# Four more weight blocks as seven products, and a solve whose transposes stay on VectorE

## The chip, the cores and the metric

The kernel runs on one core of a Trainium2 chip. The metric is the time of one execution on the device in microseconds (us). Its engines run side by side: TensorE (PE, with its weight loads as PEld), VectorE (DVE), ScalarE (ACT), GpSimd (POOL) and SyncE (SP). SP, ACT and POOL each have a queue that issues DMAs in order.

## The reference

One residual layer on 1024 tokens of width 1024. A normalised input h is projected by one wide matrix; two mixers use the parts, and gates join them:

```python
h = _rmsnorm(x, norm_w[layer])
proj = h @ w_in[layer]
dsa_qkv, dsa_z, gdn_qkv, gdn_z, gdn_b, gdn_a, gate_a, gate_b = _split_columns(proj)
...
o_a = _dilated_mixture(q_a, k_a, v_a)            # three groups of dilated window attention
y_a = (o_a * silu(dsa_z)) @ w_up_a[layer]
cqkv = silu(_causal_depthwise_conv(gdn_qkv, conv_w[layer]))      # 4 taps
gq, gk, gv = split(cqkv)                          # l2 norms on gq, gk
o_b = _gated_delta_rule(gq, gk, gv, g, beta)      # chunks of 64, a scan over 16 chunks
y_b = (_rmsnorm(o_b, gdn_norm_w) * silu(gdn_z)) @ w_up_b[layer]
merged = sigmoid(gate_a) * y_a + sigmoid(gate_b) * y_b
x = x + merged @ w_out[layer]
return _rmsnorm(x, final_norm_w)
```

In each chunk of the delta rule a unit lower triangular 64x64 matrix I + A has to be inverted for each head: t_inv = (I + A)^-1, A from the keys, beta and the decays.

## The kernel before

**Projections.** The wide matrix is cut into units of 256 columns: 18 of attention (query, key and value for three groups and two halves of the heads), 6 of the delta rule ("gdn", a half of the heads `hb` and query, key or value), 4 of z and 8 of the gates. fp32 accuracy comes from fp16 pairs: h is h_hi + h_lo, a weight block whi + wlo, and three matmuls (hi·hi, lo·hi, hi·lo; lines L184, L185, L186) make one product. A unit is done in one of two ways:
- *Normal*: four output tiles of 128 columns x 512 tokens, each 8 slices of depth x 3 matmuls of 512 columns. ScalarE makes whi (L167), VectorE wlo (L84, 128x1024), twice each. A unit is 32 steps ("ticks") of three matmuls.
- *Seven*: the unit as a 2x2 matrix of blocks, multiplied in seven products of half the depth instead of eight (a Strassen scheme, with the sums of h made once). 28 ticks. VectorE makes four sums of weight blocks (L329), and seven low halves (L84, 128x512), ScalarE seven high ones (L330). Two of the four outputs come out as -p - rest and need a pass of VectorE when they leave PSUM.

`SEVENS` lists the units done the second way.

**Order.** PE's instructions stand in the order in which the code writes them: a queue `feed` of units gives projection matmuls, and the other work calls `feed.tick(n)` to put n ticks of them between its own steps. The numbers of ticks (`STATE_LAG`, `tick(2)` and others) are set by hand. The order on all other engines, DMA issues among them, is set by a planner at the end of the program (`Step.cost`, `fill`), which goes through the program with a table of durations and fixes one order per engine. Engines wait in that order.

**After the attention** come, with the remaining units between the steps: `decay` (products gm, then exp), `keys_side` (key norms, pair products MT, and the scalars brk and rk packed for the solve), `solve`, `merge`, `state_parts`, for hb = 0 and 1, then query pairs, the scan over chunks, and the up and output projections. `solve` inverts 32x32 blocks: MT goes to DRAM and comes back as As with one matrix in each partition (4 row blocks x 32 matrices), 31 steps of two VectorE instructions (stmp, X) give the inverse X, and X goes back through DRAM (u_d) into MT. A transposed negative copy T goes through DRAM (t_d) into T1p. `merge` joins the 32x32 blocks to 64x64 on PE: left products of MT and T1p (L1353), a VectorE pass Y, right products of Y and U (L1368). The scalars `bsc` reach the solve by a PE transpose, a copy and two DMA passes through DRAM (sc_d).

**Keys.** `rope_out` copies rotated queries and keys out of their tiles into Q and K by DMAs of 32 partitions, high halves (pch, pkh) and low halves (pcl, pkl), all on SP's queue. POOL's queue carries the weight loads wstage.

Of the kernel before, what the change touches and what calls it, by code (L numbers as in the profile page):

```python
# [11 lines left out]
F32 = mybir.dt.float32  # L12
# [18 lines left out]
U_Z = 24  # L31
# [7 lines left out]
def gdn_unit(hb, what):  # L39
    return U_GDN + hb * 3 + what  # L40
# [5 lines left out]
          + [U_GATE + i for i in (0, 1, 2, 6, 7)] + [U_Z + i for i in range(4)])  # L46
# [11 lines left out]
STATE_LAG = 12  # L58
# [20 lines left out]
def hybrid_block(ctx: ExitStack, tc: tile.TileContext, A):  # L79
# [544 lines left out]
    def rope_out(pt, pieces):  # L624

        with tc.high_priority():
            for name, dst, r0, _ in pieces:
                for hd in range(4):
                    nc.sync.dma_start(out=dst[r0:r0 + 32, hd], in_=pt[name[1]][32 * hd:32 * hd + 32, "AB".index(name[0])])
# [366 lines left out]
    def conv_unit(hb, what, dst_of, then=None):  # L996

        def gen(w):
            for c in range(2):
# [3 lines left out]
                for hf in range(2):  # L1003
                    def take(p):
                        with tc.high_priority():
# [8 lines left out]
                            for j in (2, 1, 0):  # L1014
                                STT(a, xc[:, j:j + 512], cw[:, cidx, j:j + 1], a, ALU.mult, ALU.add)
                            parts = [(dst[:, 8 * hf:8 * hf + 8].rearrange("p c i -> p (c i)"), lambda x: x)]
                            if hb:

                                dv = dst[:, 8 * hf:8 * hf + 8].rearrange("p (t c) i -> p t c i", c=2)
                                parts = [(dv[:, :, b], lambda x, b=b: x.rearrange("p (t c i) -> p t c i", c=2, i=64)[:, :, 1 - b])  # L1020
                                         for b in range(2)]
                            if (hb, what) in SILU:
                                for d, of in parts:
                                    SC.activation(d, of(a), AF.Silu, scale=2.0)
                            else:
                                th = pre[0].tile([128, 512], F32, name="cth", tag="cth", bufs=2)
                                SC.activation(th, a, AF.Tanh)
                                for d, of in parts:
                                    STT(d, of(th), 1.0, of(a), ALU.add, ALU.mult)
# [6 lines left out]
        feed.add(("gdn", hb, what), Normal(A["w"][gdn_unit(hb, what)]), gen)  # L1036
# [145 lines left out]
    def decay(hb):  # L1182

        for t in range(8):
# [18 lines left out]
            feed.tick(2)  # L1203
# [23 lines left out]
    def sumsq(hb, src, dst, take=None):  # L1227

        for t0 in range(0, 8, 2):
# [11 lines left out]
            feed.tick(2)  # L1241
# [36 lines left out]
    def keys_side(hb):  # L1278
# [7 lines left out]
        for i, x in enumerate((brk, rk)):  # L1286
            V.tensor_copy(pack[:, i].rearrange("p t (e q) -> p t e q", e=2), heads_h2(x[:, :, hsl]))
# [20 lines left out]
    def solve(hb, m_d, bsc):
# [8 lines left out]
        for k in range(31):  # L1317
# [8 lines left out]
        V.tensor_scalar(T1, X.rearrange("p j i -> p i j"), -1.0, None, op0=ALU.mult)  # L1326
        u_d = tc.dram_tile([4, 32, 32, 32], F32, name=f"u_d{hb}")
        t_d = tc.dram_tile([4, 32, 32, 32], F32, name=f"t_d{hb}")
        nc.sync.dma_start(out=u_d.rearrange("k n j i -> (k n) (j i)"), in_=X.rearrange("p j i -> p (j i)"))
        nc.sync.dma_start(out=t_d.rearrange("k n j i -> (k n) (j i)"), in_=T1.rearrange("p j i -> p (j i)"))  # L1330
        U = MT[hb]
        T1p = p2_.tile([128, 8, 4, 32], F32, name="T1p", tag="T1p", bufs=1)
        for kb in range(4):
            b = kb % 2
            if b == 0:
                nc.sync.dma_start(out=T1p[32 * kb:32 * kb + 32].rearrange("p t h j -> p (t h) j"),
                                  in_=t_d[kb].rearrange("n i j -> i n j"))
# [129 lines left out]
    gate_unit(5, gate_spill)  # L1467
# [52 lines left out]
    for i in (6, 7):  # L1520
        gate_unit(i, gate_spill)
# [257 lines left out]
    feed.until(("gate", 6))  # L1779
# [179 lines left out]
QUEUE_NS = 4  # L1959
# [47 lines left out]
class Step:  # L2007
# [17 lines left out]
    def cost(self):  # L2025
# [17 lines left out]
        elif self.kind == "InstDMACopy":  # L2043
            kb = w[0].total / 1024
            rows = max(x.rows[1] - x.rows[0] for x in self.args)
            self.hold = 590 if rows <= 32 else 500 if rows <= 64 else 350
            self.ns, self.pass_ns, self.kb = 2800 + (4 if w[0].dram else 7) * kb, 60, kb
            if min(w[0].piece, r[0].piece) < 256:
                self.hold = 1400 if kb > 64 else 600
                self.ns += 2800  # L2050
            if self.eng == "POOL":
                self.hold = 530 if rows > 64 else 630
        elif self.eng == "DVE":
            one = len(r) == 1
            fast = one and not r[0].psum
            self.ns = {"InstMemset": 60 + 0.5 * n, "InstReciprocal": 150 + 6.2 * n, "InstTensorCopy": 160 + (0.55 if fast else 1.0417) * n}.get(
# [109 lines left out]
def fill(steps, rank, back, given):  # L2166
# [4 lines left out]
    free, moved, due, open_ = [{e: x() for e in order} for x in (float, float, list, list)]  # L2171
# [201 lines left out]
```

## Time and profile before

| | us |
|---|---|
| median of 3 runs (1048.63 to 1051.87) | 1049.8 |
| the profiled execution | 1048.82 |
| its span, first to last instruction | 1047.0 |
| PE busy | 1029.0 (98%) |
| VectorE busy | 885.7 (85%) |
| ScalarE busy | 583.0 (56%) |
| POOL busy | 56.1 (5%) |

The granted TensorE clock was 0.998. A matmul row has the time until its last result is written, and rows overlap, so PE's busy share says that it always has something in flight, not that it runs at its peak. The profile is of one execution, and the stages it names are read by the time from the span's start.

### The profile page before, as it was taken

The numbers are of one execution on the slowest core, as the hardware profiler recorded it, in microseconds if no ns is written. First come the engines' busy times: TensorE is split into PE (matmuls) and PEld (weight loads), VectorE is DVE, ScalarE is ACT, GpSimd is POOL, SyncE is SP. The second block draws the span as 40 slices with busy tenths as digits, with TensorE's granted clock in tenths as the row PEclk, the third lists the DMA queues.
The fourth block names the chain that finished last, engine by engine and source line by source line (L and its number), as shares of the span: only waits on it lengthen the run. The fifth ranks groups of instructions, "written<-read, shape, count | busy, mean of one in ns | idle before, by whom it ended". The sixth has DMA issues, their size and how long they took to land.

```text
span 1047.0 us, 24924 instructions
## 1 busy us (share of the span) xinstructions
PE 1029.0 (98%) x9962; PEld 632.9 (60%) x9962; DVE 885.7 (85%) x2052; ACT 583.0 (56%) x1322; POOL 56.1 (5%) x107
## 2 busy tenths in 40 slices
PE   6999999999999999999999999999999999999997
PEld 5995595775966855876655545545555555444444
DVE  6898988979979889989998897976588768899934
ACT  6455767777767766667756633344444345344523
POOL 0000000000000000010010000110100001000000
PEclk9999999999999999999999999999999999999999
DMA  8144531542624622470146357794874415743232
GB/s 284 64 129 114 138 112 62 152 112 78 186 84 116 165 91 74 118 201 28 43 161 183 113 134 202 258 278 150 266 254 152 142 62 176 288 124 117 67 115 81
DMA packets 99780, 148.53 MB, mean 142 GB/s; under 512 B 31168, under 2 KB 64704, under 8 KB 98512
## 3 DMA queue, kind: packets, MB, share of 16 engines
q1 hardware_dynamic: 69264, 84.64, 27.9%
q0 software_dynamic: 12320, 44.11, 13.4%
q10 hardware_dynamic: 18080, 18.20, 5.0%
q8 instruction: 78, 1.28, 0.5%
q14 instruction: 38, 0.31, 0.1%
HBM read 91.13 MB, written 36.90 MB: 122 GB/s over the span
## 4 chain that ended last, share of the span: by engine, by line
PE 84%; DVE 10%; ACT 2%; DMA 1%; issue 1%; SPq 0%; DVEq 0%; ACTq 0%
PE ps_mm L184 21%; PE ps_mm L186 20%; PE ps_mm L185 20%; PE ps_G L813 2%; PE ps_S L186 2%; PE ps_S L185 2%; PE ps_S L184 2%; DVE ca L84 1%; PE ps_S L790 1%; PE ps_S L792 1%; PE ps_G L185 1%; PE ps_G L186 1%; PE ps_G L184 1%; DVE sm L799 1%; DVE tl L87 1%
## 5 line engine op out<-in xcount | busy, mean ns | idle before, releaser
L186 PE MATMUL ps_mm<-h_hi,wlo 128*128 128x512 f16 (+1 forms) x504 | 189.3, 376 | 0.0
L184 PE MATMUL ps_mm<-h_hi,whi 128*128 128x512 f16 (+1 forms) x436 | 163.8, 376 | 0.0
L185 PE MATMUL ps_mm<-h_lo,whi 128*128 128x512 f16 (+1 forms) x436 | 163.5, 375 | 0.0
L186 PEld LDWEIGHTS <-wlo 128*128 128x128 f16 x748 | 73.2, 98 | 81.4
L184 PEld LDWEIGHTS <-whi 128*128 128x128 f16 x816 | 79.9, 98 | 65.7
L185 PEld LDWEIGHTS <-whi 128*128 128x128 f16 x816 | 79.9, 98 | 64.4
L803 ACT ACTIVATE sm<-sm,osb 128x128 f32<-128x128 f32 (+1 forms) x160 | 69.3, 434 | 34.9 <-DVE osb L799 33.3
L330 ACT ACTIVATE whi<-wstage 128x512 f16<-128x512 f32 x84 | 51.1, 626 | 30.0 <-DVE wstage L329 11.9
L799 DVE CUSTOM_DVE_ANT_0 sm<-ps_S,amask 128x128 f32<-128x128 f32 (+1 forms) x192 | 60.3, 345 | 6.6 <-PE ps_S L792 6.5
L87 DVE TENSOR_TENSOR tl<-ps_G,th 128x256 f16<-128x256 f32 (+1 forms) x96 | 51.7, 539 | 13.3 <-ACT th L818 13.0
L84 DVE SCALAR_TENSOR_TENSOR whi<-wstage,whi 128x512 f16<-128x512 f32 x84 | 57.2, 684 | 4.6 <-ACT whi L330 4.4
L329 DVE TENSOR_TENSOR wstage<-wstage 128x512 f32<-128x512 f32 x84 | 56.9, 685 | 0.8
L185 PE MATMUL ps_mm<-wlo,h_hi 128*128 128x256 f16 (+1 forms) x256 | 57.3, 246 | 0.0
L84 DVE SCALAR_TENSOR_TENSOR ca<-xc,cw,ca 128x512 f32<-128x512 f32 x72 | 53.7, 745 | 3.8 <-ACT ca L1013 3.3
L184 PE MATMUL ps_mm<-h_hi,wlo 128*128 128x512 f16 x136 | 51.6, 380 | 0.0
L185 PE MATMUL ps_mm<-h_lo,wlo 128*128 128x512 f16 x136 | 51.5, 379 | 0.0
L84 DVE SCALAR_TENSOR_TENSOR wlo<-wstage,whi 128x1024 f16<-128x1024 f32 x38 | 46.1, 1218 | 6.3 <-ACT whi L167 5.6
L818 ACT CAST th<-ps_G 128x256 f16<-128x256 f32 (+1 forms) x96 | 44.0, 458 | 12.5 <-PE ps_G L813 10.8
L813 PE MATMUL ps_G<-cons,sm 128*128 128x128 f32 x280 | 46.9, 274 | 1.3 <-ACT sm L803 1.2
L84 DVE SCALAR_TENSOR_TENSOR wlo<-wstage,wlo 128x512 f16<-128x512 f32 x63 | 42.4, 683 | 6.2 <-ACT wlo L330 6.2
L313 POOL DMA_DIRECT2D wstage<-in_w x42 | 22.2, 530 | 473.2 <-DVE whi L84 154.9
L184 PE MATMUL ps_mm<-whi,h_hi 128*128 128x256 f16 (+1 forms) x192 | 46.5, 256 | 0.0
(492 smaller groups left out, 2950.3 us busy)
## 6 DMA issues: line engine op xcount, KB each, us to landing
wstage<-in_w POOLq DMA_DIRECT2D x68, 512.0 KB, 4.5
og<-osb ACTq DMA_DIRECT2D x32, 132.0 KB, 2.2
og<-og SPq DMA_DIRECT2D x32, 132.0 KB, 2.4
sga<-gspa SPq DMA_DIRECT2D x8, 512.0 KB, 9.1
wstage<-in_w_up POOLq DMA_DIRECT2D x8, 512.0 KB, 5.3
sgb<-gspb SPq DMA_DIRECT2D x8, 512.0 KB, 4.2
wos<-in_w_out SPq DMA_DIRECT2D x8, 512.0 KB, 4.7
xr<-in_x SPq DMA_DIRECT2D x8, 512.0 KB, 4.1
```

Source lines behind the costliest of these rows:

```text
L84: (eng or V).scalar_tensor_tensor(out, in0, scalar, in1, op0=op0, op1=op1)
L87: (eng or V).tensor_tensor(out, in0, in1, op)
L184: PE.matmul(out, lhsT=wh(k), rhs=mh(k), start=first and i == 0, stop=False, skip_group_check=True)
L185: PE.matmul(out, lhsT=wh(k), rhs=ml(k), start=False, stop=False, skip_group_check=True)
L186: PE.matmul(out, lhsT=wl(k), rhs=mh(k), start=False, stop=last and i == len(ks) - 1, skip_group_check=True)
L313: nc.gpsimd.dma_start(out=st, in_=self.src[n])
L329: V.tensor_tensor(self.part[name], self.part[x], self.part[y], ALU.add)
L330: SC.activation(t[:, b, 0], self.part[name], AF.Copy, scale=W_SCALE)
L799: V.tensor_tensor_reduce(P[:, u, :128 * nk], psc[:, u * 256:u * 256 + 128 * nk], mask, -cexp, -NEG, ALU.add, ALU.min, accum_out=osb[:, 256 ...
L803: SC.activation(P[:, u, :128 * nk], P[:, u, :128 * nk], AF.Exp, bias=osb[:, 256 + hd:257 + hd], scale=-1.0, accum_out=osb[:, 260 + hd:261 ...
L813: PE.transpose(pt[:, c:c + 128], P[:, u, i * 128:i * 128 + 128], ident)
L818: SC.copy(th[:, :n], pt[:, :n])
```

## The change

Five parts, in one diff:
1. Four more units become *Seven*: gates 3, 4 and 5 and the gdn query unit of hb = 1. For the latter `conv_unit` gets a `gen7`; the filter's part is moved into a function. Gate 6 moves ahead of the z units. The numbers of ticks are made fewer by 16 in `decay`, `sumsq` and `STATE_LAG`, as the four units have 16 ticks fewer.
2. T1p is written by one VectorE transpose of 32x32 blocks from X; T, t_d and its DMAs are gone. The sign is put into brk (times -1) and the solve's step adds.
3. bsc is written by a VectorE transpose from pack; the PE transpose, packT, sc_d and its DMAs are gone.
4. The pieces of U come back in the order 1, 3, 0, 2. Low key pieces are issued by POOL instead of SP.
5. The planner's table: one DMA path shared by all queues instead of one for each, with other prices, and a price for the transpose.

```diff
 SEVENS = ([att_unit(g, hs, w) for g in (1, 0) for hs in range(2) for w in range(3)]
-          + [U_GATE + i for i in (0, 1, 2, 6, 7)] + [U_Z + i for i in range(4)])
+          + [gdn_unit(hb, w) for hb, w in [(1, 0)]] + [U_GATE + i for i in (0, 1, 2, 3, 4, 5, 6, 7)] + [U_Z + i for i in range(4)])
-STATE_LAG = 12
+STATE_LAG = 8
...
-                    nc.sync.dma_start(out=dst[r0:r0 + 32, hd], in_=pt[name[1]][32 * hd:32 * hd + 32, "AB".index(name[0])])
+                    eng = nc.gpsimd if name[1] == "l" and not twice else nc.sync
+                    eng.dma_start(out=dst[r0:r0 + 32, hd], in_=pt[name[1]][32 * hd:32 * hd + 32, "AB".index(name[0])])
...
+        def gen7(w):
+            dst, edge, held = {}, {}, []
+
+            def shifted(c, hf, p, rest):
+                xc = pre[0].tile([128, 515], F32, name="xc", tag="xc", bufs=2)
+                if hf == 0:
+                    V.memset(xc[:, 0:3], 0.0)
+                if rest is None:
+                    SC.copy(xc[:, 3:515], p)
+                else:
+                    STT(xc[:, 3:515], p, -1.0, rest, ALU.mult, ALU.subtract)
+                ...
+            yield from seven_products(w, out)
+        add_unit(("gdn", hb, what), gdn_unit(hb, what), gen, gen7)
...
-            feed.tick(2)                       # decay
+            feed.tick(2 - (hb ^ (t > 3)))
-            feed.tick(2)                       # sumsq
+            feed.tick(1 + hb)
...
-            V.tensor_copy(pack[:, i].rearrange("p t (e q) -> p t e q", e=2), heads_h2(x[:, :, hsl]))
+            V.tensor_scalar(pack[:, i].rearrange("p t (e q) -> p t e q", e=2), heads_h2(x[:, :, hsl]),
+                            (-1.0, 1.0)[i], None, op0=ALU.mult)
+        bsc = p2_.tile([128, 2, 32], F32, name="bsc", tag="bsc", bufs=2)
+        V.transpose(bsc.rearrange("p a i -> p (a i)"), pack.rearrange("p a t h -> p (a t h)"))
...
-        PE.transpose(pp[0:64, 0:128], pack.rearrange("p a t h -> p (a t h)"), ident)
-        SC.copy(packT, pp[0:64, 0:128])
-        ... sc_d written and read by three DMAs
...
-            TT(X[:, :k + 1, k + 1:], X[:, :k + 1, k + 1:], tv, ALU.subtract)
+            TT(X[:, :k + 1, k + 1:], X[:, :k + 1, k + 1:], tv, ALU.add)
         TT(X, X, bsc[:, 1, None, :].to_broadcast([128, 32, 32]), ALU.mult)
-        T1 = p2_.tile([128, 32, 32], F32, name="T1", tag="As", bufs=1)
-        V.tensor_scalar(T1, X.rearrange("p j i -> p i j"), -1.0, None, op0=ALU.mult)
-        ... t_d written and read by three DMAs
+        T1p = p2_.tile([128, 8, 4, 32], F32, name="T1p", tag="T1p", bufs=1)
+        V.transpose(T1p.rearrange("p t h j -> p j (t h)"), X)
-        for kb in range(4):
+        for kb in (1, 3, 0, 2):
...
-QUEUE_NS = 4
-            self.ns, self.pass_ns, self.kb = 2800 + (4 if w[0].dram else 7) * kb, 60, kb
+            self.kb = max(3.07 * kb, 1.6 * w[0].total / min(w[0].piece, r[0].piece))
+            self.ns, self.pass_ns = 3000 + 1.3 * self.kb, 60
-            moved[e] = max(moved[e], t) + s.kb * QUEUE_NS
+            moved = max(moved, t + 2000) + s.kb
```

The end of the solve of hb = 0 on VectorE; ca and vT belong to the filter of a value unit, which runs beside it. Before:

```order
L87 TENSOR_TENSOR stmp<-As,X 128x60
L87 TENSOR_TENSOR X<-X,stmp 128x30x2
L87 TENSOR_TENSOR stmp<-As,X 128x31
L87 TENSOR_TENSOR X<-X,stmp 128x31
L87 TENSOR_TENSOR X<-X,bsc 128x1024
L84 SCALAR_TENSOR_TENSOR ca<-xc,cw,ca 128x512
L1326 TENSOR_SCALAR T_9060<-X 128x1024
L84 SCALAR_TENSOR_TENSOR ca<-xc,cw,ca 128x512 x2
```

After:

```order
L87 TENSOR_TENSOR X<-X,stmp 128x31
L87 TENSOR_TENSOR X<-X,bsc 128x1024
L84 SCALAR_TENSOR_TENSOR ca<-xc,cw,ca 128x512
L1363 STREAM_TRANSPOSE T1p<-X 128x32x32
L87 TENSOR_TENSOR rv<-ps_O,bg 128x512
L84 SCALAR_TENSOR_TENSOR ca<-xc,cw,ca 128x512
L87 TENSOR_TENSOR As<-As,bsc 128x1024
```

The transpose stands where T stood, and the next solve's first instruction (As) follows it three places on.

SP's queue at the same place: u_d and t_d are the ways of X and T out, MT and T1p their ways back, As the matrices of the next solve, rv_d values on their way to DRAM. Before:

```order
L1329 DMA u_d_9062<-X 128x1024
L1330 DMA t_d_9063<-T_9060 128x1024
L1338 DMA MT_8581<-u_d_9062 32x32x32
L1336 DMA T1p<-t_d_9063 32x32x32 x2
L1338 DMA MT_8581<-u_d_9062 32x32x32
L1311 DMA As<-m_d_9433 128x1024
```

After:

```order
L1348 DMA As<-m_d_9376 128x1024
L1365 DMA u_d_9015<-X 128x1024
L1485 DMA rv_d<-rv 128x4x128
L1369 DMA MT_8581<-u_d_9015 32x32x32 x4
L1426 DMA rvt<-rv_d 128x4x256
```

As is now issued ahead of u_d, and T's three issues are gone.

POOL's queue about the last key block (Ks; L313 are loads of Seven units, L163 of Normal ones). Before:

```order
L313 DMA wstage<-in_w 128x1024 x26
L163 DMA wstage<-in_w 128x1024 x4
L313 DMA wstage<-in_w 128x1024 x4
L163 DMA wstage<-in_w 128x1024 x2
L1315 MEMSET X 128x1024
```

After:

```order
L313 DMA wstage<-in_w 128x1024 x6
L163 DMA wstage<-in_w 128x1024 x3
L630 DMA Ks<-pcl 32x1024 x8
L163 DMA wstage<-in_w 128x1024
L313 DMA wstage<-in_w 128x1024 x4
L163 DMA wstage<-in_w 128x1024
```

The eight low pieces of that key block stand behind the third of four loads of Normal units.

More of the change, by code (lines that the diff above doesn't have):

```diff
@@ L1013, in take @@
                             SC.activation(a, p, AF.Copy, scale=cw[:, cidx, 3:4])
[L1014 to L1029, printed above, removed]
+                            filtered(c, hf, xc, a, dst, cidx)
                         last.append(xc)
@@ L1034, in gen, with finish, out @@
                     yield from proj(w, c, hf, take)
-        feed.add(("gdn", hb, what), Normal(A["w"][gdn_unit(hb, what)]), gen)
+        def gen7(w):
[6 more added lines that the diff above has]
+                    SC.copy(xc[:, 3:515], p)
+                else:
+                    STT(xc[:, 3:515], p, -1.0, rest, ALU.mult, ALU.subtract)
+                if hf == 0:
+                    edge[c] = pre[0].tile([128, 4], F32, name="edge", tag="edge", bufs=2)
+                    V.tensor_copy(edge[c][:, 0:3], xc[:, 512:515])
+                return xc
+            def finish(c, hf, xc):
+                cidx = 4 * what + 2 * hb + c
+                if c not in dst:
+                    dst[c] = dst_of(c)
+                if hf:
+                    V.tensor_copy(xc[:, 0:3], edge[c][:, 0:3])
+                a = pre[0].tile([128, 512], F32, name="ca", tag="ca", bufs=2)
+                SC.activation(a, xc[:, 3:515], AF.Copy, scale=cw[:, cidx, 3:4])
+                filtered(c, hf, xc, a, dst[c], cidx)
+                if hf and then:
+                    then(c, dst[c])
+            def out(c, hf, p, rest):
+                with tc.high_priority():
+                    xc = shifted(c, hf, p, rest)
+                    if (c, hf) == (1, 1):
+                        held.append(xc)
+                        return
+                    finish(c, hf, xc)
+                    if (c, hf) == (1, 0):
+                        finish(1, 1, held[0])
+            yield from seven_products(w, out)
+        add_unit(("gdn", hb, what), gdn_unit(hb, what), gen, gen7)
     kT, pre = [], []
@@ L1778, in hybrid_block @@
             feed.tick(4)
-    feed.until(("gate", 6))
+    feed.until(("z", "b", 1))
     feed.tick(1)
@@ L2170, in fill @@
     start, order = [0.0] * len(steps), {e: [] for e in ENGINES.values()}
-    free, moved, due, open_ = [{e: x() for e in order} for x in (float, float, list, list)]
+    free, due, open_ = [{e: x() for e in order} for x in (float, list, list)]
+    moved = 0.0
     events, wake, table, small, end = [], {}, 0, None, 0.0
@@ L2234, in fill @@
         if s.kb and not back:
-            moved[e] = max(moved[e], t) + s.kb * QUEUE_NS
-            late = max(0, moved[e] + 1200 - t - s.ns)
+            moved = max(moved, t + 2000) + s.kb
+            late = max(0, moved + 300 - t - s.ns)
         end = max(end, t + late + s.ns)
```

47 lines of the change are left out of this document (25 added, 22 removed).

## The prediction

> **What bounds the kernel now.** I read the page first, its busy line and the shares of the chain that ended last:
>
> ```profile
> PE 1029.0 (98%) x9962; PEld 632.9 (60%) x9962; DVE 885.7 (85%) x2052; ACT 583.0 (56%) x1322; POOL 56.1 (5%) x107
> PE 84%; DVE 10%; ACT 2%; DMA 1%; issue 1%; SPq 0%; DVEq 0%; ACTq 0%
> ```
>
> TensorE is the chain, and VectorE (DVE) is its one other large part. Next I asked for busy times by stage: projections and attention to 545, decay and solve of block 0 to 645 (its merge), solve of block 1 to 714 (its merge), the last pair products to 760, the scan to 857, the rest.
>
> ```profile
> 0.00:400.00 400.00, 391.15 (x3875) 285.29 (x3876) 351.51 (x799) 267.60 (x663) 17.74 (x37) 1.00 0.43 124
> 400.00:545.00 145.00, 144.34 (x1413) 95.62 (x1412) 140.99 (x449) 98.12 (x252) 5.83 (x12) 1.00 0.36 103
> 545.00:645.00 100.00, 98.97 (x778) 52.16 (x778) 86.00 (x167) 51.25 (x89) 8.18 (x16) 1.00 0.57 160
> 645.00:714.00 69.00, 68.37 (x942) 36.19 (x937) 58.61 (x120) 26.10 (x46) 8.33 (x14) 1.00 0.83 260
> 714.00:760.00 46.00, 46.00 (x784) 26.11 (x780) 25.79 (x44) 18.82 (x35) 7.53 (x13) 1.00 0.60 193
> 760.00:857.00 97.00, 97.00 (x1320) 50.43 (x1317) 75.01 (x188) 39.70 (x69) 4.22 (x8) 1.00 0.50 159
> ```
>
> The columns are span, PE, weight loads, DVE, ACT, POOL, clock, DMA share and GB/s. PE is busy in every stage, so work taken from it shortens the program, if VectorE can follow. VectorE has 4 us idle in 400 to 545 (145 - 140.99), and 14.0 and 10.4 us in the two stages that the change loads. Its busy time there is the number to watch.
>
> **The matmuls taken away.** A block of weights as four plain products is 4 x 8 x 3 = 96 matmuls of 512 columns; as seven products of half the depth it is 7 x 4 x 3 = 84. Four blocks change (gates 3, 4, 5 and the second query block), so 48 matmuls go; the order of the changed program has just 48 fewer. A matmul reads 0.38 us, but they overlap; the price is from start to start (timeline of PE inside a plain block):
>
> ```profile
> 618.79 0.38 PE L184 MATMUL ps_mm<-h_hi,whi 128*128 128x512 f16 x1
> ...
> 624.83 0.38 PE L185 MATMUL ps_mm<-h_lo,whi 128*128 128x512 f16 x1
> ```
>
> 28 steps in 6.04 us are 0.216 us each, so 48 x 0.216 = 10.4 us. The two transposes of the solve scalars, no longer on PE, are some 0.2 us more. Term: **-10.6 us**, all of it on the path. By the order, 12 of the matmuls and the transposes lie ahead of the merge of block 0 (2.8 us), 38 ahead of the merge of block 1 (8.4 us: two gate blocks, and STATE_LAG's four ticks fewer), the rest further on.
>
> **What VectorE and ScalarE get in exchange** (groups of instructions; eviction and T from their rows):
>
> ```profile
> L84 DVE SCALAR_TENSOR_TENSOR whi<-wstage,whi 128x512 f16<-128x512 f32 x84 | 57.2, 684 | 4.6 <-ACT whi L330 4.4
> L329 DVE TENSOR_TENSOR wstage<-wstage 128x512 f32<-128x512 f32 x84 | 56.9, 685 | 0.8
> L84 DVE SCALAR_TENSOR_TENSOR wlo<-wstage,wlo 128x512 f16<-128x512 f32 x63 | 42.4, 683 | 6.2 <-ACT wlo L330 6.2
> L84 DVE SCALAR_TENSOR_TENSOR wlo<-wstage,whi 128x1024 f16<-128x1024 f32 x38 | 46.1, 1218 | 6.3 <-ACT whi L167 5.6 <-ACT qT L1213 0.5
> L330 ACT ACTIVATE whi<-wstage 128x512 f16<-128x512 f32 x84 | 51.1, 626 | 30.0 <-DVE wstage L329 11.9 <-PE ps_mm L186 10.2 <-PE ps_mm L185 6.5
> L1326 DVE TENSOR_SCALAR T<-X 128x1024 f32<-128x1024 f32 x2 | 2.1, 1045 | 0.0
> 554.82 0.68 DVE L84 SCALAR_TENSOR_TENSOR gst<-ps_mm,x 128x512 f32<-128x512 f32 x1
> ```
>
> Each block gains 4 sums, 4 and 3 low halves and 2 evictions that subtract, and loses 2 low halves of 1024: 4 x 0.685 + 4 x 0.684 + 3 x 0.683 + 2 x 0.68 - 2 x 1.218 = 6.45 us, 25.8 us for four. ScalarE gains about 7 x 0.626 a block less two of 1024; it is busy half the time in both stages, which hides it. The trace has no VectorE transpose. Its nearest row by size is T, 1.045 us, which it replaces one for one; X times its scalars, the row at 626.45 below, is 1.22. I take 1.2 and hold 2.5 (twice that) as the dear end, 0.7 as the cheap one: 0.2 us more twice, between -0.7 and +2.9 us.
>
> [...]
>
> **Where it collides: the merges.** Both solves must end before PE reaches the merges:
>
> ```profile
> 545.29 3.70 DVE L87 TENSOR_TENSOR gm<-wide,cons 128x512 f16<-128x512 f16 x6
> 626.45 1.22 DVE L87 TENSOR_TENSOR X<-X,bsc 128x1024 f32<-128x1024 f32 x1
> 627.74 0.34 SPq L1329 DMA_DIRECT2D u_d<-X  x1
> 629.33 0.34 SPq L1330 DMA_DIRECT2D t_d<-T  x1
> 632.32 0.93 SPq L1336 DMA_DIRECT2D T1p<-t_d  x2
> 640.38 0.50 SPq L1338 DMA_DIRECT2D MT<-u_d  x1
> 644.43 1.13 PE ps_S L1353 x64
> 645.61 1.41 DVE L87 TENSOR_TENSOR Y<-ps_S,pack 32x512 f32<-32x512 f32 x2 [2.27 <-PE ps_S L1353]
> 713.17 1.13 PE ps_S L1353 x64
> 714.64 1.41 DVE L87 TENSOR_TENSOR Y<-ps_S,pack 32x512 f32<-32x512 f32 x2
> ```
>
> Before, T goes out and comes back by two DMAs between 629.33 and the merge at 644.43. The transpose on VectorE writes T1p directly: the left products need no DMA, and of U's pieces the two that the right products need are issued first. PE now comes to this merge at 644.43 - 2.8 = 641.6, X was ready at 627.7, so the solve of block 0 may end several us later and still be in time. The scalars' DMA round trip, which is also gone, stood beside the keys' own transfer; I cost it at nothing.
>
> The tight place is the first Y of block 1. From the first gm it has 714.64 - 545.29 = 169.4 us now, of which VectorE idles 24.4 (14.0 + 10.4). Afterwards PE arrives 8.4 us sooner. By the order VectorE has ahead of that Y 14 more sums, 14 + 11 more low halves, 6 more evictions, 8 fewer long low halves, 4 fewer filter steps and one fewer reduction (these come later now): 39 x 0.684 + 6 x 0.68 - 8 x 1.22 - 4 x 0.745 - 0.69 + 0.4 = 17.7 us. 24.4 - 8.4 - 17.7 = -1.7 us: without help VectorE would be late by 1.7 us plus whatever it still waits for.
>
> Help comes from the order itself. Two steps of the solve that follow each other directly cost more than with another instruction between them:
>
> ```profile
> 592.94 0.24 DVE L87 TENSOR_TENSOR stmp<-As,X 128x87 f32<-128x87 f32 x1
> 593.10 0.68 DVE L1240 TENSOR_REDUCE kss<-ps_S 128x8 f32<-128x512 f32 x1
> 624.88 0.25 DVE L87 TENSOR_TENSOR stmp<-As,X 128x87 f32<-128x87 f32 x1
> 625.16 0.25 DVE L87 TENSOR_TENSOR X<-X,stmp 128x87 f32<-128x87 f32 x1
> ```
>
> The same step takes 0.16 us with an independent follower and 0.28 with a dependent one. Ahead of that Y the order had 95 such dependent neighbours and has 42: 53 x 0.12 = 6.4 us. And right products come one pause after the left ones, which gives Y some 2 us. So VectorE may still wait -1.7 + 6.4 + 2 = 6.7 us between 545 and 714 and lose PE nothing. Some waits stay, since what they wait for is not moved (a bank of PE, a pass of ScalarE):
>
> ```profile
> 549.72 0.69 DVE L87 TENSOR_TENSOR gm<-wide,cons 128x512 f16<-128x512 f16 x1 [0.72 <-PE ps_G L1198]
> 551.34 0.69 DVE L87 TENSOR_TENSOR gm<-wide,cons 128x512 f16<-128x512 f16 x1 [0.93 <-PE ps_G L1198]
> 557.72 0.69 DVE L84 SCALAR_TENSOR_TENSOR x<-ps_mm,x 128x512 f32<-128x512 f32 x1 [1.61 <-PE ps_mm L186]
> 582.51 2.33 DVE L84 SCALAR_TENSOR_TENSOR ca<-xc,cw,ca 128x512 f32<-128x512 f32 x3 [0.70 <-ACT ca L1013]
> ```
>
> These four are 4 us, the floor. The ceiling is all 24.4, but the 2.27 us ahead of Y at 645.61 and others like it fall where VectorE had run out of work, and now it has more. I take 10, nearer the floor: a loss of **+3.3 us**, between 0 and 17.7.
>
> **Low key pieces on POOL's queue.** 48 issues leave SP. Between attention blocks each waits on nothing soon needed. The one near place is the last key block, whose eight now stand on POOL behind the third weight load:
>
> ```profile
> 452.50 0.53 POOL L163 DMA_DIRECT2D wstage<-in_w  x1 [4.39 <-DVE sml L87]
> 452.55 2.67 SPq L629 DMA_DIRECT2D Ks<-pcl  x4
> L790 PEldq EVENT_SEMAPHORE  x4: 51/51/51, 460.7 to 461.1; - x4
> L1437 POOL DMA_DIRECT2D un_d<-uw x16: 631/631/659, 666.7 to 737.7; - x16
> ```
>
> SP now issues the last ones until 455.2. On POOL they start at 453.0 and take 8 x 0.63 (the nearest row, a copy of 64 rows) to 458.1; PE asks for them near 461. Landing in 2 to 6 us makes a stall of 0 to 3: **+0.5 us**. The weight load behind them was issued at 458.76 and isn't delayed.
>
> [...]
>
> **The sum.** -10.6 + 3.3 + 0.5 = -6.8 us on the profiled execution of 1048.8 (span 1047.0 and 1.8 around it): 1042.0. The median of the runs, 1049.8, stands 1.0 above that execution; the planner's new DMA prices also reorder the first 545 us, but PE idles only 0.7 us of the last 145 of them, so that little is to be won there and I give it nothing. The forecast is **1042.0 us**.
>
> **Rivals.**
> (a) VectorE hides everything: it waits 7 us or less, the last key block costs nothing. -10.6 gives 1038.2, and with the small stalls ahead of the merges gone 1037. For it: VectorE's added work is independent of the solve. Chance 0.27.
> (b) VectorE is the bound from 545 to 740: it still waits 14 to 17 us, so 7 to 10 are lost, -10.6 + 8.5 + 0.5 = -1.6: 1047 to 1048, no difference. Against it: most idle stood where it lacked work. Chance 0.1.
> (c) Slower: the merge of block 1. All 24.4 us of waits remain, since the order is fixed and each wait in it stays. 24.4 - 6.7 = 17.7 lost, -10.6 + 17.7 = +7.1: 1056. It decides from 17.3 us of waits on. Chance 0.06.
> [...] Chance 0.02.
> (e) The forecast, waits of 7 to 14 us, 1038.5 to 1046: chance 0.55, own range 1039 to 1045.
>
> **How the numbers follow.** A measurement of this kernel tells about 0.3%, 3.1 us: faster is below 1046.7. Cases (a) and (e): 0.82; within, (b): 0.1; slower, (c) and (d): 0.08. The range 1036.5 to 1047 leaves out (c), (d), most of (b) and a tenth below.
>
> **What would show it.** Right: PE's L184 to L186 groups with 48 fewer matmuls; VectorE near 911 us busy, and over 93% of the stage from the first gm to the merge of block 1; T1p transposes near 1.2 us, no t_d or sc_d transfers; PE losing a few us near the merges, put down to Y or its predecessors on VectorE. Wrong: transposes over 2.5 us, POOL issues over 1 us, PE stalls before 545 that were not there, or waits of VectorE over 17 us ahead of the second merge.

## The result and the profile after

| | before | changed |
|---|---|---|
| median of the runs, us | 1049.3 (1048.63 to 1051.87) | 1044.0 (1043.78 to 1045.11) |
| the profiled execution, us | 1048.82 | 1043.78 |
| its span, us | 1047.0 | 1042.0 |

Each side has four runs here; the table ahead of the prediction had three of the kernel before. The ratio is 0.9946, with a 95% interval of 0.9934 to 0.9959: 5.3 us faster by the medians, 5.0 by the two profiled executions. The forecast was 1042.0. The page of the changed kernel, its busy line and the shares of its chain:

```profile
PE 1021.4 (98%) x9912; PEld 627.9 (60%) x9912; DVE 905.0 (87%) x2100; ACT 595.1 (57%) x1350; POOL 79.9 (8%) x155
PE 71%; DVE 5%; issue 3%; DMA 2%; ACT 1%; POOL 0%; DVEq 0%; POOLq 0%; ACTq 0%
```

TensorE has 50 instructions less, the 48 matmuls and two transposes. The same stages as in the prediction, in the changed kernel (columns: span, PE, weight loads, DVE, ACT, POOL, clock, DMA share, GB/s):

```profile
400.00:545.00 145.00, 144.36 (x1420) 95.53 (x1419) 140.99 (x449) 97.47 (x250) 9.28 (x18) 1.00 0.36 103
545.00:645.00 100.00, 98.94 (x799) 52.26 (x798) 95.79 (x200) 56.97 (x102) 7.64 (x15) 1.00 0.50 141
645.00:714.00 69.00, 69.00 (x1043) 36.75 (x1041) 67.90 (x136) 33.85 (x59) 9.34 (x16) 1.00 0.79 245
714.00:760.00 46.00, 43.22 (x636) 23.47 (x637) 29.48 (x50) 22.06 (x42) 8.06 (x14) 0.96 0.76 246
```

In the two stages of the solves VectorE is idle for 4.2 and 1.1 us (it was 14.0 and 10.4), and TensorE loses nothing more there than before (1.1 us idle in the two, it was 1.7). The loss stands in the next stage: TensorE is idle for 2.8 us of 714 to 760, and the mean granted clock is 0.96. The left products of the two merges (timeline of PE, first and third group) start 1.3 and 7.8 us sooner than before, where the prediction had 2.8 and 8.4, so at 705 most of the saving is there. Before, then after:

```profile
644.36 1.20 PE L1353 MATMUL ps_S<-T1p,MT 32*32 32x32 f32 x64
...
713.10 1.20 PE L1353 MATMUL ps_S<-T1p,MT 32*32 32x32 f32 x64
```

```profile
643.06 1.11 PE L1384 MATMUL ps_S<-T1p,MT 32*32 32x32 f32 x58
...
705.33 1.20 PE L1384 MATMUL ps_S<-T1p,MT 32*32 32x32 f32 x64
```

Where it goes, first on PE (timeline; L1294 turns queries into the bank ps_O for the query sums):

```profile
743.77 0.66 PE L1294 MATMUL ps_O<-cons,qT 128*128 128x128 f32 x4 [0.48 <-DVE rq L1298]
...
748.67 0.77 PE L1294 MATMUL ps_O<-cons,qT 128*128 128x128 f32 x4 [2.30 <-DVE rq L1298]
749.24 0.63 PE L184 MATMUL ps_mm<-sum4h,whi 128*128 128x512 f16 x1
749.66 0.63 PE L185 MATMUL ps_mm<-sum4l,whi 128*128 128x512 f16 x1
...
752.57 0.38 PE L186 MATMUL ps_mm<-sum4h,whi 128*128 128x512 f16 x1
```

PE waits 0.48 and 2.30 us for the sum rq, which frees the bank. Then its matmuls take 0.63 us, with 0.43 from start to start, until 752.57: eight steps in 3.33 us in place of 1.73, another 1.6 us. The clock shows it (stretches of two microseconds, same columns):

```profile
746.00:748.00 2.00, 0.37 (x2) 0.00 (x0) 1.97 (x4) 0.60 (x1) 0.00 (x0) 1.00 0.03 12
748.00:750.00 2.00, 1.33 (x6) 0.80 (x7) 1.87 (x4) 1.67 (x3) 0.31 (x1) 0.77 0.34 131
750.00:752.00 2.00, 2.00 (x6) 0.73 (x5) 1.90 (x7) 0.06 (x1) 0.00 (x0) 0.50 0.66 200
```

And why rq is late, on VectorE (timeline):

```profile
743.03 0.68 DVE L1298 TENSOR_REDUCE rq<-ps_O 128x8 f32<-128x512 f32 x1
745.99 0.69 DVE L329 TENSOR_TENSOR wstage<-wstage 128x512 f32<-128x512 f32 x1 [2.28 <-DMA wstage<-in_w]
746.60 0.69 DVE L84 SCALAR_TENSOR_TENSOR whi<-wstage,whi 128x512 f16<-128x512 f32 x1
747.32 0.69 DVE L329 TENSOR_TENSOR wstage<-wstage 128x512 f32<-128x512 f32 x1
747.93 0.68 DVE L1298 TENSOR_REDUCE rq<-ps_O 128x8 f32<-128x512 f32 x1
```

The third sum rq stands in VectorE's fixed order behind a sum of weight blocks, and that one waits for a weight load. The chain of the changed kernel names the load:

```profile
734.97 10.93 DMA wstage<-in_w
...
748.67 0.77 PE ps_O L1294 x4
```

The load was issued at 734.97 and took 10.93 us; the profile page's median for such a load is 4.5. The DMA engines were full: their share from 725 to 745 is 0.97. The kernel before is at the same place of the program 7.8 us later, so its stretch is 733 to 753, with 0.84 (first row after, second before).

```profile
725.00:745.00 20.00, 19.52 (x332) 11.24 (x331) 10.43 (x17) 8.99 (x16) 4.67 (x8) 1.00 0.97 312
```

```profile
733.00:753.00 20.00, 20.00 (x336) 11.78 (x333) 7.92 (x12) 7.25 (x13) 4.67 (x8) 1.00 0.84 273
```

There two weight loads, issued at 745.39 and 746.99, took 6.8 to 7.1 us to land; ScalarE waited 0.8 us for one of them, and TensorE not at all. What is closer together now is the stores of a gate's spills (gspb): the four of one gate are issued within 12.1 us, from 721.3 to 733.5, and took 23.3 us before.

### The profile page after: what moved, and what is told of

The parts are those of the page before. It is cut to its first block, busy times and chain, and to the rows that moved or that the text cites. A ratio compares the mean times of both kernels' runs of the same rounds, so it can differ in the third digit from the quotient of the medians.

```text
span 1042.0 us, 24958 instructions
## 1 busy us (share of the span) xinstructions
PE 1021.4 (98%) x9912; PEld 627.9 (60%) x9912; DVE 905.0 (87%) x2100; ACT 595.1 (57%) x1350; POOL 79.9 (8%) x155
## 4 chain that ended last, share of the span: by engine, by line
PE 71%; DVE 5%; issue 3%; DMA 2%; ACT 1%; POOL 0%; DVEq 0%; POOLq 0%; ACTq 0%
PE ps_mm L184 17%; PE ps_mm L185 17%; PE ps_mm L186 17%; DMA wstage<-in_w 2%; PE ps_G L814 2%; PE ps_S L184 1%; PE ps_S L185 1%; PE ps_S L186 1%; PE ps_S L791 1%; PE ps_S L793 1%; PE ps_G L184 1%; PE ps_G L186 1%; PE ps_G L185 1%; PE ps_S L1745 1%; PE ps_G L1773 1%
## 5 line engine op out<-in xcount | busy, mean ns | idle before, releaser
L186 PE MATMUL ps_mm<-h_hi,wlo 128*128 128x512 f16 (+1 forms) x408 | 152.9, 375 | 0.0
L184 PE MATMUL ps_mm<-h_hi,whi 128*128 128x512 f16 (+1 forms) x324 | 121.2, 374 | 0.0
L185 PE MATMUL ps_mm<-h_lo,whi 128*128 128x512 f16 (+1 forms) x324 | 121.1, 374 | 0.0
L184 PEld LDWEIGHTS <-whi 128*128 128x128 f16 x752 | 73.8, 98 | 59.1 <-issue 0.8
L185 PEld LDWEIGHTS <-whi 128*128 128x128 f16 x752 | 73.7, 98 | 59.1 <-issue 1.8
L330 ACT ACTIVATE whi<-wstage 128x512 f16<-128x512 f32 x100 | 61.1, 626 | 42.0 <-PE ps_mm L186 14.4
L84 DVE SCALAR_TENSOR_TENSOR whi<-wstage,whi 128x512 f16<-128x512 f32 x100 | 68.0, 683 | 4.6 <-ACT whi L330 4.3
L329 DVE TENSOR_TENSOR wstage<-wstage 128x512 f32<-128x512 f32 x100 | 68.4, 684 | 3.1 <-DMA wstage<-in_w 2.3
L184 PE MATMUL ps_mm<-h_hi,wlo 128*128 128x512 f16 x168 | 63.9, 380 | 0.0
L185 PE MATMUL ps_mm<-h_lo,wlo 128*128 128x512 f16 x168 | 63.7, 379 | 0.0
L313 POOL DMA_DIRECT2D wstage<-in_w x50 | 26.7, 534 | 437.3 <-DVE osb L800 68.6
L186 PEld LDWEIGHTS <-whi 128*128 128x128 f16 x336 | 33.0, 98 | 40.2 <-issue 0.8
L330 ACT ACTIVATE wlo<-wstage 128x512 f16<-128x512 f32 x75 | 46.3, 628 | 14.4 <-DVE wstage L329 9.5
```

What stands on the lines that cost most here:

```text
L84: (eng or V).scalar_tensor_tensor(out, in0, scalar, in1, op0=op0, op1=op1)
L184: PE.matmul(out, lhsT=wh(k), rhs=mh(k), start=first and i == 0, stop=False, skip_group_check=True)
L185: PE.matmul(out, lhsT=wh(k), rhs=ml(k), start=False, stop=False, skip_group_check=True)
L186: PE.matmul(out, lhsT=wl(k), rhs=mh(k), start=False, stop=last and i == len(ks) - 1, skip_group_check=True)
L313: nc.gpsimd.dma_start(out=st, in_=self.src[n])
L329: V.tensor_tensor(self.part[name], self.part[x], self.part[y], ALU.add)
```

## The experiments

My theory after this reading: the 10.4 us of matmuls are all there, and the missing part is one place, 742 to 753, where a query sum waits behind a weight load that the full DMA engines delay. The rivals were: VectorE has too much work (then the pause moves elsewhere); the load is slow because of POOL's queue; the saving itself is smaller; the other parts of the change cost something.

In the runs with "held" orders, the planner makes its orders as for the changed kernel, and only the named instructions are moved in the finished lists. In all other runs it plans anew, and one moved DMA then gives new orders on all engines. Ratios are to runs of the kernel before on the same chip.

**1. One query sum moved ahead of the weight sum (VectorE's order held).**

```diff
-L329 wstage<-wstage;  L84 whi<-wstage,whi;  L329 wstage<-wstage;  L1298 rq<-ps_O
+L1298 rq<-ps_O;  L329 wstage<-wstage;  L84 whi<-wstage,whi;  L329 wstage<-wstage
```

> The changed kernel with one place in VectorE's fixed order moved: the third query sum (rq, L1298 of the changed kernel) stands directly behind the second, ahead of the weight sum (L329) that waits for a load. All other orders are as in the changed kernel. Theory A (the stall at 746 is VectorE's order: a query sum that TensorE waits for stands behind a sum that waits for a late weight load, and the half clock follows from the stall): the wait of 2.46 us at 746 falls under 0.7, the matmuls after it step by 0.216 us and not 0.43, and the time falls by 3 to 4.5 us, to 1039.5 to 1041. Theory B (the weights themselves are late, so TensorE only waits at another place): the pause moves to the next product, which needs the block of that load, near 747 to 749, and the gain is under 1.2 us: 1042.8 to 1044. Theory C (VectorE has too much work there): the same as B, and VectorE shows no wait between 742 and 750.

Measured: median 1042.8 us (1041.52 to 1048.17), ratio 0.9938 (0.9916 to 0.9961); profiled span 1039.7, 2.3 below the changed kernel's. This profile is of the fastest of six executions; two took 1046.9 and 1048.2 us, at a mean clock of 0.996 and 0.995 where the other four read 0.998 or 0.999, so the half clock may have followed in those two. The waits of TensorE from 700 to 760, in the order time, times, longest:

```profile
PE ps_O L1294 <- DVE rq L1298: 1.4, 1, 1.4
PE ps_mm L184 <- DVE gst L84: 1.0, 1, 1.0
```

By its median (1042.8) it is at the lower end of theory B, by its profile between the theories: no half clock followed there (clock 1.00 from 742 to 757), but 1.4 us of the wait remained at an earlier step and 1.0 came back nine microseconds later. So the order of VectorE is a part of the cause, and the late weights are the other.

**2. Two other loads moved out of the full stretch (all else held).**

```diff
 (SP's list)
-L1568 sga2<-gspa2;  L1568 sga3<-gspa3        (issued at 735.1)
 L1726 kdec ... L1535 oa x2                   (15 loads of the first scan chunks)
+L1568 sga2<-gspa2;  L1568 sga3<-gspa3
```

> The changed kernel with two loads of SP's queue moved: sga 2 and 3 (512 KB each, L1568, now issued at 735.1) stand 15 places later, behind the loads of the first scan chunks. All other orders are as in the changed kernel. Theory A (the weight load issued at 734.97 takes 10.93 us because the DMA engines are full from 735 to 745, at 413 GB/s, 1 MB of it these two loads): with 1 MB less, 2.4 us at 413 GB/s, it lands some 2.4 us sooner, near 743.5, the stall of 2.46 us at 746 falls under 0.7, no half clock follows, and the time falls by 3 to 4.5 us, to 1039.5 to 1041. [...]

Measured: 1039.5 us (1039.11 to 1041.76), ratio 0.9900 (0.9884 to 0.9916). The two weight loads, min, median and max from issue to landing, in the changed kernel and then in this run:

```profile
DMA to landing us min/median/max: 8.4/9.7/10.9
```

```profile
DMA to landing us min/median/max: 7.7/8.0/8.4
```

The second load landed 2.5 us sooner after its issue, VectorE does not wait for it, and the pause and the half clock are gone (VectorE's timeline, and two stretches, of this run):

```profile
743.04 0.68 DVE L329 TENSOR_TENSOR wstage<-wstage 128x512 f32<-128x512 f32 x1
743.64 0.69 DVE L84 SCALAR_TENSOR_TENSOR whi<-wstage,whi 128x512 f16<-128x512 f32 x1
744.36 0.69 DVE L329 TENSOR_TENSOR wstage<-wstage 128x512 f32<-128x512 f32 x1
744.97 0.68 DVE L1298 TENSOR_REDUCE rq<-ps_O 128x8 f32<-128x512 f32 x1
```

```profile
746.00:748.00 2.00, 2.00 (x13) 1.05 (x12) 1.00 (x2) 1.96 (x4) 0.31 (x1) 1.00 0.38 73
...
750.00:752.00 2.00, 2.00 (x11) 0.87 (x9) 1.66 (x6) 0.41 (x1) 0.00 (x0) 1.00 1.03 335
```

Theory A: 4.7 us of span (1042.0 to 1037.3) for moving two loads that nobody there needs. POOL issues the late load at nearly the same time (734.54 and 734.97), so its queue is not the cause. From the left products of the second merge to the first product of the scan (ps_G<-vn,kdec) the changed kernel takes 52.1 us (705.3 to 757.4) and this run 48.0 (704.8 to 752.8): 4.1 of the 4.7 us are won there. The other 0.6 stand ahead of the first merge, where nothing was moved, so they belong to the spread between executions.

**3. The first part alone taken out (planned anew).**

```diff
-          + [gdn_unit(hb, w) for hb, w in [(1, 0)]] + [U_GATE + i for i in (0, 1, 2, 3, 4, 5, 6, 7)] + ...
+          + [U_GATE + i for i in (0, 1, 2, 6, 7)] + ...
-STATE_LAG = 8
+STATE_LAG = 12
 (ticks of decay and sumsq and gate 6's place as before)
```

> The changed kernel without its first part: gates 3 to 5 and the second query block are plain products again, with the numbers of ticks and the place of gate 6 as before; VectorE's transposes, the queue of the low keys and the planner's prices stay. 48 matmuls more than the changed kernel, 10.4 us at 0.216 us. Theory A (the saving is TensorE's matmuls alone; the other parts are worth within 1.5 us of nothing, and the stall at 743 to 753 belongs to the new units): 1048 to 1050, within 0.15 per cent of the kernel before, and no half clock. Theory B (the transposes shorten the solves and pay by themselves: the pauses of 0.8 and 0.9 us near 586 and 650 go): 1046.5 to 1048. Theory C (the planner's prices or the keys cost the first 1.1 us and more): 1050 to 1052.

Measured: 1050.0 us (1048.73 to 1051.71), ratio 0.9999 (0.9990 to 1.0009). Theory A, at the upper edge of its range (1048 to 1050). The other parts together give nothing by themselves. From here to run 2 on the same chip are 10.5 us, and 48 x 0.216 is 10.4.

**4 and 5. The low key pieces back on SP's queue, first with the other orders held, then planned anew.**

```diff
-                    eng = nc.gpsimd if name[1] == "l" and not twice else nc.sync
+                    eng = nc.sync
```

> The changed kernel with the low key pieces back on SP's queue (eight behind each eight high ones); the orders of VectorE, ScalarE and of all other DMAs are held as in the changed kernel. Theory A (the queue of the keys is worth nothing, and the 1.1 us that the changed kernel loses near 210 to 224 come from the new order of VectorE there): the time stays within 0.7 us of 1044 and the small pauses at 218 and 224 stay. Theory B (the keys on POOL delay the weight loads behind them, which costs the 1.1 us): the pauses go and the time falls by about 1 us, to 1043. Theory C (SP becomes late with the queries or the last key block): 1045 to 1047, with a pause near 461.

> The changed kernel with the low key pieces issued by SP again, and all orders planned anew for it (in the run before, the orders were held, and SP's eight low pieces stood behind all eight high ones: 1056.8 us, TensorE waiting for Ks at 224 to 228 and later). Theory A (POOL's queue is worth little where the planner may place the pieces itself, as in the kernel before, which had no pause for Ks): within 2 us of 1044, no pause over 1 us before 545, the stall near 746 as in the changed kernel. Theory B (VectorE now makes the low pieces too late for one queue, so POOL's queue is needed): pauses at L791 put down to Ks, 1047 to 1057.

Measured: 1056.8 us (1052.77 to 1060.82), ratio 1.0059 (1.0036 to 1.0083), held; 1047.1 us (1043.71 to 1053.84), ratio 0.9971 (0.9952 to 0.9990), planned anew. Held, TensorE waits for the keys themselves near 221 to 230:

```profile
PE ps_S L791 <- DMA Ks<-pcl: 3.1, 3, 2.2
```

and there are pauses of 1.7 to 2.6 us near 304, 476 and 483 too; behind those at 228, 304 and 483 the matmuls ran at half clock (mean clock 0.52 from 230 to 234, 0.69 from 304 to 308, 0.63 from 482 to 486). Planned anew, TensorE never waits for Ks; pauses of 1.4 and 0.6 us near 220 follow from a weight load. The first run took theory C, far above its number. The second has the time of theory B (its lower end) without B's waits for Ks, so neither theory holds. Held, the run is 11.9 us slower than the changed kernel by the ratios, which is the price of a list with eight low pieces behind eight high ones. Planned anew, 2.6 us by the ratios (0.9971 against 0.9946) are lost, but the intervals overlap: that POOL's queue is worth something is not shown. The small pauses at 218 and 224 of the changed kernel, which cost it up to 1.1 us at the first gm, are there in the held run as well, so the queue isn't their cause.

**6. The planner's DMA prices of before (planned anew).**

```diff
-            self.kb = max(3.07 * kb, 1.6 * w[0].total / min(w[0].piece, r[0].piece))
-            self.ns, self.pass_ns = 3000 + 1.3 * self.kb, 60
+            self.ns, self.pass_ns, self.kb = 2800 + (4 if w[0].dram else 7) * kb, 60, kb
...
-            moved = max(moved, t + 2000) + s.kb
+            moved[e] = max(moved[e], t) + s.kb * QUEUE_NS
... (and the old times that an issue holds its queue)
```

> The changed kernel with the planner's DMA prices of before (each queue with a path of its own). TensorE's order is the same; the orders of the other engines are planned anew. Theory A (the prices are worth nothing, as the prediction gave them): 1042 to 1046. Theory B (the one shared path is needed now that the DMA engines are full near 735 to 745): another weight load arrives late, pauses over 1 us somewhere between 545 and 770, 1046 to 1052. Theory C (the new prices cost the 1.1 us near 210 to 224 and made the order with the stall at 746): both go, 1038.5 to 1041.

Measured: 1049.7 us (1047.10 to 1052.91), ratio 0.9993 (0.9982 to 1.0004). Theory B by its time and its pauses, though the late transfer is not a weight load but a piece of U. TensorE's waits from 640 to 765:

```profile
PE ps_G L1399 <- DMA MT<-u_d: 5.0, 1, 5.0
PE ps_O L1294 <- DVE rq L1298: 2.7, 1, 2.7
```

With the old prices the pieces of U go out when the DMA engines are full (share 0.97 from 640 to 650 in this run) and one of them lands 12.6 us after its issue, where the changed kernel's landed after 3.2 to 4.2. The granted clock read 0.50 from 653.35 to 660.17 (a mean of 0.67 from 650 to 660), from inside the pause of 5.0 us on. Without the new prices nothing is left of the whole gain (4.9 us by the ratios), while run 3, which has them, shows that they are worth nothing without the units.

**7. The solve through DRAM again, on top of run 2 (planned anew).**

```diff
-        V.transpose(T1p.rearrange("p t h j -> p j (t h)"), X)
+        V.tensor_scalar(T1, X.rearrange("p j i -> p i j"), -1.0, None, op0=ALU.mult)
+        ... t_d written and read, sc_d written and read, the scalars turned by PE
```

> The run sga_held (1039.5 us) with the solve as in the kernel before: T and the scalars go through DRAM again (t_d, sc_d) and TensorE turns the scalars, the pieces of U come in the order 0 to 3; the four units as seven products stay. Orders planned anew, the two sga loads moved as in sga_held. Theory A (in the changed kernel the first left product starts 11.4 us after the transposition of T1p ends at 693.9, so the solve has slack for the way through DRAM, which took some 15 us from X to the merge before): 0 to 4 us are lost ahead of the merge of block 1, 1039.5 to 1043.5. Theory B (with TensorE 8.4 us earlier at that merge the round trip is what it waits for): a pause of 5 to 10 us at L1384 or the first Y, 1044 to 1050.

Measured: 1043.6 us (1042.01 to 1047.47), ratio 0.9937 (0.9923 to 0.9952), at the upper end of theory A, 3.9 us above run 2 by the ratios. The profile is of its slowest execution (1047.47). TensorE's waits from 640 to 765, the two longest:

```profile
PE ps_mm L184 <- DVE gst L84: 1.7, 1, 1.7
PE ps_S L1397 <- DMA T1p<-t_d: 1.6, 2, 1.3
```

The wait for T1p is there, 1.3 us at the merge of block 1, with matmuls at half clock behind it (mean clock of the execution 0.997). It is no large part; the rest is the other pauses of a new plan, which this run doesn't separate.

**8. One more query sum moved, on top of run 2 (held).**

> The run sga_held with one more place moved: in VectorE's order the second query sum of block 1 stands directly behind the first, ahead of a weight's low half and a weight sum. Theory A (the pause of 0.62 us that is left at 742 is again VectorE's order): the pause goes, 1038.8 to 1039.3. Theory B (the weights are needed at once, so the pause moves): within 0.3 us of sga_held, 1039.2 to 1039.8. Either is beside the measurement; the trace decides.

Measured: 1041.2 us (1040.61 to 1041.64), ratio 0.9915 (0.9902 to 0.9928), on another chip than run 2. Neither theory: the pause grew, 2.5 us in two waits, and from the second merge to the scan are 50.3 us. What is new in its trace is ScalarE (timeline; ACTq rows are its DMA issues):

```profile
729.01 3.46 ACTq L1465 DMA_DIRECT2D wn_d<-ws  x2
732.51 0.63 ACT L330 ACTIVATE whi<-wstage 128x512 f16<-128x512 f32 x1 [3.04 <-issue]
```

Two issues took 3.46 us here (1.60 in the changed kernel's profile), and ScalarE did nothing meanwhile. The high half behind them frees the buffer that the weight load needs, so that load was issued at 735.20 and not at 732.71 as in run 2.

**9, 10 and 11. The changed kernel and run 2 again on one chip, and the four wn_d stores of block 1 issued by SP (all else as in run 2).**

```diff
-                        nc.scalar.dma_start(out=w_d[ts, c2, :, 2 * hb:2 * hb + 2]...
+                        (nc.sync if hb else nc.scalar).dma_start(out=w_d[ts, c2, :, 2 * hb:2 * hb + 2]...
```

> The changed kernel once more, on the chip of the next two runs, since runs of one kernel spread by up to 4 us where the DMA engines are full, and the changed kernel had only four. All theories: a median of 1043.5 to 1045.5. Theory A (what is lost near 746 hangs on when one load lands, and the half clock follows it in some executions only): a spread of 2 us or more. Theory B (the loss is fixed by the orders): a spread under 1 us.

> The run sga_held once more, on the chip of the run before this one. Theory A (its gain of 4.5 us over the changed kernel is the stall and the half clock at 742 to 753): 1039 to 1041, 3.5 to 5 us below the changed kernel on the same chip. Theory B (it was the chip): less than 2 us below.

> The run sga_held with four more DMAs moved: the four stores wn_d of block 1 (L1465) are issued by SP, which has nothing else from 707 to 749, and not by ScalarE, where issuing two of them took 1.1 to 3.5 us while the DMA engines were full, ahead of the high half of a weight (L330) that frees the buffer of the late load. VectorE's and POOL's orders and the rest of ScalarE's are as in sga_held. Theory A (ScalarE's blocked issues delay the weight load in its turn): the load that was issued at 732.7 goes out 1 to 2 us sooner, the pause of 0.62 us at 742 goes, 1038 to 1039.3. Theory B (the DMA engines are full in any case, so an earlier issue lands no earlier): within 0.5 us of sga_held. Theory C (the stores now wait in SP's queue and the scan's first loads come late): a pause near 757, 1040 to 1043.

Measured: the changed kernel 1042.6 us (1042.14 to 1044.34), ratio 0.9926 (0.9910 to 0.9943); run 2 again 1040.0 us (1039.58 to 1041.82), ratio 0.9904 (0.9887 to 0.9921); with the stores on SP 1040.1 us (1039.12 to 1040.73), ratio 0.9901 (0.9885 to 0.9917). The changed kernel's median is 0.9 us below the expected range, its spread of 2.2 us is theory A's, and its profiled execution (1044.34) has the same stall and half clock (0.83 from 745 to 755 in both). On this chip run 2 gains 2.6 us by the medians, between the two theories; by the profiled spans 2.5. Two things make it smaller than 4.5. The half clock follows only in some executions, to judge by the mean clock, which 3.41 us at 0.50 lower by 0.0016: it is 0.997 in the two of 1043.74 and 1044.34 us, and 0.998 or 0.999 in the three of 1042.14 to 1042.56, while all four executions of the first measurement had 0.997. And in the two profiles run 2 is 1.1 us later already at the first merge, behind a pause of 1.4 us between 460 and 480, far ahead of the moved loads. From the second merge to the scan it takes 48.8 us and the changed kernel 52.4, so 3.6 us are won where the loads were moved, against 4.1 before. The stall shrank from 2.3 to 1.1 us and the half clock went (1.00 from 745 to 755). With the stores on SP, ScalarE's high half came at 729.11 and was no longer held up by them (a wait of 0.31 us, for TensorE), SP took 7.86 us from the first of the four issues to the last, and the load went out at 732.00, against 732.71 in run 2 and 734.43 in its repetition. Waits of 0.9 and 0.7 us remain, and the time is that of run 2: theory B.

The best versions are run 2 and run 11, 1.0% below the kernel before and, by the ratios, 0.2 to 0.5% below the changed one.

## Why the prediction was right, and what in it was wrong

The forecast of 1042.0 lies 2.0 us below the first median and 0.6 below the second, and both are inside the range. That the number fits is luck. The loss of some 5 us is the size of case (e), and it came from elsewhere: by its condition (VectorE waits 7 us or less) the outcome is rival (a), whose 1038.2 run 2 nearly reaches with 1039.5. Two terms that were too dear stood in for one that was missing.

**The matmuls, -10.6.** Right. 50 fewer instructions on PE, and run 3 against run 2 gives 10.5 us. A part is lost early: the first gm comes at 546.4, 1.1 us later than before, behind small pauses near 218 and 224, which the prediction had named as a sign of being wrong.

**VectorE's work.** The 25.8 us are there: the groups of sums and halves grew by what was counted (lines of the changed kernel; before, these had 84, 84 and 63):

```profile
L329 DVE TENSOR_TENSOR wstage<-wstage 128x512 f32<-128x512 f32 x100 | 68.4, 684 | 3.1 <-DMA wstage<-in_w 2.3
L84 DVE SCALAR_TENSOR_TENSOR whi<-wstage,whi 128x512 f16<-128x512 f32 x100 | 68.0, 683 | 4.6 <-ACT whi L330 4.3
L84 DVE SCALAR_TENSOR_TENSOR wlo<-wstage,wlo 128x512 f16<-128x512 f32 x75 | 50.7, 683 | 9.2 <-ACT wlo L330 8.8
L1363 DVE STREAM_TRANSPOSE T1p<-X 128x1024 f32<-128x1024 f32 x2 | 3.9, 1974 | 0.0
L1334 DVE STREAM_TRANSPOSE bsc<-pack 128x64 f32<-128x64 f32 x2 | 0.5, 234 | 0.0
```

But VectorE's total is 905.0, not the 911 that I asked for. The rows of all its groups add up to 28 us more than before (25.8, and 2.3 for the transposes), while the busy time, which counts overlapping rows once, grew by 19.3. A row of 0.68 us can be followed by the next after 0.60, as the list of run 2 shows (743.04 and 743.64), so the price of 0.684 was too high for a part of the added work. The 6.4 us of dependent neighbours, which the prediction worked out for the merges and left out of this total, belong to the difference as well; how the 9 us divide isn't separated.

**The transposes.** Mis-sized: 1.97 us, not 1.2, inside the range of 0.7 to 2.5. It took 1.9 times T, the pass of 1.045 us that it replaced. It cost nothing on the path: TensorE has no wait for T1p.

**The merges, +3.3.** Wrong: 0. VectorE waited 5.3 us between 545 and 714, less than the 6.7 that my own sum allowed. The step that failed is "I take 10, nearer the floor": I took four waits as a floor of 4 us, and kept 6 of the other 20 us. The waits for ScalarE's passes nearly went, from 12.7 to 1.3 us by the longest rows; that the work put between them did it is my reading, which no run tests. VectorE's waits from 545 to 714, two of the kernel before and one of the changed:

```profile
DVE rq L1254 <- ACT ps_O L1253: 4.3, 2, 2.2
DVE ca L84 <- ACT ca L1013: 3.3, 5, 1.3
```

```profile
DVE ca L84 <- ACT ca L1032: 0.5, 1, 0.5
```

VectorE is busy for 157 of the 162 us from 545 to the second merge, so it is near its bound there, as the prediction said; the price at that bound was rival (a)'s.

**The low key pieces, +0.5.** 0 at the last key block: TensorE has no wait for Ks. POOL's issues were shorter than my nearest row of 631 to 659 ns:

```profile
L630 POOL DMA_DIRECT2D Ks<-pcl x40: 496/496/516, 141.1 to 455.7; - x40
```

That row also settles (d), to which the prediction gave 0.02: no run shows an issue of POOL held up by VectorE. VectorE is busy for 298.68 of the 330 us from 130 to 460, in which all 40 stand, and the longest of them took 516 ns. What I missed is that the orders now count on that queue: with them held, taking it away costs 11.9 us (run 4). What the queue is worth when all is planned anew stays open (run 5).

**The planner's prices, nothing.** Wrong: undone, they cost 4.9 us by the ratios, nearly all that the change gives (run 6). I judged them by the first 545 us, where PE idled little; they matter at 640 to 660, where run 6 waits for U, and at 742 to 753.

**What the sum had no term for.** In place of 3.3 + 0.5 us at the merges and keys stand 4.4 us at 742 to 753 (2.8 of pauses, 1.6 of half clock), of which run 2 won back 3.6 to 4.1, and the 1.1 us ahead of the first gm. With these, -10.6 + 4.4 + 1.1 = -5.1, and the two profiled executions differ by 5.0. I read the DMA share of 714 to 760 in the stage table (0.60 before) and asked nothing of it. The table alone would not have shown it: over the whole stage the share is 0.76 after and 0.75 before at the same place of the program (722 to 768). It is the 20 us of 0.97, and an order of VectorE in which a query sum stands behind the load that came late in them. The expectation "PE losing a few us near the merges, put down to Y or its predecessors" is the sentence that the trace refutes.

## What to carry to other kernels

Where TensorE was the chain, matmuls taken away came off the time one for one (10.5 us from run 3 to run 2, for 10.4 of matmuls), and less where the DMA engines were full (5.3 us in the changed kernel, at a share of 0.97 from 725 to 745). So when a stage gets shorter, ask for its DMA share in short stretches as well as for the next engine's busy time: loads that took 7 us at a share of 0.84 took up to 11 at 0.97, and the first thing to move is a load that is issued early only because its queue was free. In a fixed order, an instruction that another engine waits for should not stand behind one that waits for a DMA. A change whose parts are worth nothing alone can still need all of them: here the planner's prices cost 4.9 us when undone, and the transposes 3.9 on top of run 2, though together the other parts gained nothing without the new units. Each of these runs has a new plan on all engines, and how much of its price is that plan's isn't separated.

## What the runs showed of the hardware

A pause of TensorE can cost more than its length. After seven of the pauses of over 1 us in these profiles (without the first 60 us) the matmuls ran at half clock, in the changed kernel those of 512 columns at 0.43 us from start to start instead of 0.216. The granted clock read 0.50 there, for 3.41 us in five of the seven (749.07 to 752.48 in the changed kernel; one in run 9, two in run 4, one in run 7) and for 6.83, twice as long, in the other two (653.35 to 660.17 in run 6, and 227.02 to 233.84 in run 4). The mean clocks agree: 0.997 in the changed kernel, run 7 and run 9, 0.995 in run 6 and 0.992 in run 4, against 0.998 or 0.999 in the other profiles. Length alone doesn't decide: 1.3 us was enough at the merge of run 7 and 1.7 near 304 in run 4, while 2.7 us in run 6, 2.2 near 750 in run 5 (mean clock 0.999) and 1.9 near 476 in run 4 (1.00 from 474 to 482) had no such tail. What does decide is not shown by these runs.

Issuing a DMA from ScalarE is not free. A store gspb takes 0.33 us to issue in a quiet stretch, and took 1.29 in the changed kernel at 725.89, right behind two stores wn_d; in run 11, where those are on SP, it took 0.33 at the same place. Two stores wn_d of block 1 took 0.93 to 1.23 us in the kernel before (at 735.61 and 729.60), and 0.98 to 3.46 from 724 to 733 in the changed kernel and its held runs, where the DMA share is near 1 (0.99 from 725 to 730 in the changed kernel); behind the second pair ScalarE stood idle for 1.71 us in run 9 and 3.04 in run 8, with no wait that the profile shows ("issue" in its rows). The time differed by execution, and in run 8 it set when the next weight load could start.
